# Output blocks and the next stage's first weights taken stream by stream; adaLN vectors summed on VectorE

## The chip, the cores and the metric

The kernel runs on one core of one Trainium2 chip. The metric is the device time of one execution in microseconds (us). Of the kernel before, three runs are shown: 2384.11, 2387.55 and 2390.22 us, median 2387.55 us.

## The reference, cut to what matters

The network has two layers over 512 tokens of width 1024: 256 latent tokens (called stream 0 here) and 256 context tokens (stream 1). A layer is a feed-forward block (FFN), a token mixer with three branches, and a second FFN; after each of them comes a LayerNorm of alpha * h + w * gate * f(u). Its input is modulated by adaLN vectors, nine per stream and layer, which are a matrix product of the conditioning vector with `ada_w`.

```python
u = modulate(h, mod[0], mod[1])                    # u * (1 + scale) + shift
a, b = split(u @ w_in); y = (silu(a) * b) @ w_out  # FFN, 2816 hidden columns
h = layer_norm(alpha * h + 0.5 * gate * y, g, b)   # mean and variance over the 1024 features of a token
```

In the last layer the context stream ends after the mixer's projections, so from there on only 256 tokens are computed.

## The kernel before, in words

Activations lie with features on the 128 partitions and tokens along the free axis: `u` is eight pairs of tiles (high part `uh`, low part `ul`, 128 x 512), one pair for each 128 features. Each product in float32 precision is three TensorE matmuls: weight high by `u` high, weight low by `u` high, weight high by `u` low (`mm3`, lines 139 to 143, and `projO`, lines 523 to 535). A weight of 128 x 1024 comes by one DMA into one of three `raw` buffers; `wload` (lines 120 to 133) splits it into a high part on ScalarE (line 130) and a low part on VectorE (line 132), into rings of three buffers each.

`ffn` (line 466) runs twice over 11 of the 22 blocks of hidden columns; for each block it multiplies two weights (line 530 and on), applies silu and product (lines 476 and 477), and after the 11 blocks it multiplies the eight output blocks `d` (line 516), 33 matmuls each over all 512 tokens. `residual` (line 361) adds each output block to `ah` and, in the second half, adds up the sum `s1` and the sum of squares `s2` over the features.

`norm` (line 391) then needs the sums over all eight blocks. Its TensorE work is written in a fixed order behind the last output matmul (`manual_schedule`, line 414): sums over the partitions by one-column matmuls (`token_mean`, line 388), the mean spread over all partitions (line 423), and 1/std spread by `bcast` (line 457). ScalarE, VectorE and GpSimd make the variance and the power (lines 424 to 426), VectorE subtracts the mean (line 411) and multiplies by 1/std (line 438), `mod` modulates (lines 348 to 352), `low` makes the low part (line 357), GpSimd makes the next `ah` (line 449). Only then can the next stage's first weights be multiplied. I call the stretch from the last output matmul to the first of those matmuls a hole; there are six norms: after FFN, mixer, FFN in layer 0 and the same in layer 1.

The adaLN vectors fill the holes. `ada_w` is cut into 18 groups of 512 columns per layer. `ada_group` (line 286) multiplies a group on TensorE, eight matmuls with the vector as the stationary operand, four transposes and a reduction (lines 293, 321, 322); `HOLES` says how many pieces go where in `norm`, and three groups stand in most holes. `ada_pairs` (line 250) does two groups in another way, in the background of an FFN: VectorE adds up weight times scalar (line 266, 28 instructions a pair), TensorE adds over the partitions (line 273) and transposes. `pull` (line 171) hands out the background's steps after blocks, `SKIP` leaves the first three out. The first three weights after a hole (the heads) share their steps over the eight `k`: each step has six matmuls by `uh` and then three by `ul`.

All loads go out on SyncE's queue (SP). The order of what is not fixed by hand is set by a scheduler at build time.

## Time and profile before

| | us |
|---|---|
| median of three runs | 2387.55 |
| the profiled execution, its own time | 2383.82 |
| its span, first to last instruction | 2382.0 |
| mean granted TensorE clock, share of full | 0.994 |

The profiled execution lies 3.7 us below the median, its span 1.8 us below its own time. A page counts the busy time of each engine, slices the span in 40, and lists groups of instructions; views of the trace give instructions in order of time. A matmul's row gives its time from start to end; successive matmuls overlap, so what one costs is read from the distance of two starts.

### The profile page before, as it was taken

The page shows a single profiled execution, that of the slowest core. Times are in us where ns is not written, and L with a number is a line of the kernel's source. Part 1 is how long each engine was busy: PE and PEld are TensorE (multiplying, and loading weights), DVE is VectorE, ACT ScalarE, POOL GpSimd, SP SyncE. Part 2 cuts the span into 40 slices and gives each one's busy share as a digit, 9 for nine tenths or more (in the row PEclk, how much of TensorE's full clock was granted, in tenths as well). Part 3 has the DMA queues.
Part 4 walks back from the last instruction along what each step waited for, and adds up shares of the span by engine and source line. Part 5 has one row for each costly group of instructions (what it writes and reads, how often), then busy time and mean ns, then how long its engine had stood idle before and what let it go on. Part 6 is the DMA issues. An engine that isn't in the chain of part 4 may idle for free.

```text
span 2382.0 us, 34116 instructions
## 1 busy us (share of the span) xinstructions
PE 2343.4 (98%) x13112; PEld 1971.4 (83%) x13112; DVE 1440.5 (60%) x2403; ACT 970.3 (41%) x1663; POOL 170.3 (7%) x158
## 2 busy tenths in 40 slices
PE   8999999999999999999999999999999999999998
PEld 4778778699888888867888877878887999998998
DVE  3647848656877665776433357363346687776555
ACT  3424324444654433343222234222225466645443
POOL 1003002210010000010000001000002111000000
PEclk9999999999999999999999999999999999999999
DMA  9435734723223445765332247243224344694564
GB/s 365 139 102 172 233 97 121 263 67 105 77 80 128 154 137 190 254 207 156 108 121 93 83 139 251 90 149 106 92 86 137 118 129 138 197 320 153 171 198 125
DMA packets 153314, 360.41 MB, mean 151 GB/s; under 512 B 16576, under 2 KB 38208, under 8 KB 153152
## 3 DMA queue, kind: packets, MB, share of 16 engines
q1 hardware_dynamic: 153152, 358.24, 46.2%
q8 instruction: 103, 1.69, 0.3%
q14 instruction: 59, 0.48, 0.1%
HBM read 331.96 MB, written 26.21 MB: 150 GB/s over the span
## 4 chain that ended last, share of the span: by engine, by line
PE 94%; DMA 2%; DVE 2%; ACT 1%; issue 1%; SPq 1%; POOL 0%; ACTq 0%; DVEq 0%
PE pj L530 18%; PE pj L531 18%; PE pj L533 18%; PE pj L141 7%; PE pj L143 7%; PE pj L142 7%; PE ph L632 2%; PE pj L551 1%; PE pj L552 1%; PE pj L553 1%; PE ph L293 1%; PE pa L1006 1%; PE pa L873 1%; PE ph L678 1%; PE pa L997 1%
## 5 line engine op out<-in xcount | busy, mean ns | idle before, releaser
L132 DVE TENSOR_TENSOR lo<-raw,hi 128x1024 fp32r<-128x1024 f32 (+1 forms) x455 | 524.6, 1154 | 451.1 <-ACT hi L130 450.2
L530 PE MATMUL pj<-uh,hi 128*128 128x512 f32 (+1 forms) x2096 | 752.5, 359 | 4.6 <-ACT uh L352 3.0
L533 PE MATMUL pj<-ul,hi 128*128 128x512 f32 (+1 forms) x2096 | 749.2, 358 | 1.1 <-DVE ul L357 1.1
L531 PE MATMUL pj<-uh,lo 128*128 128x512 f32 (+1 forms) x2096 | 749.5, 358 | 0.0
L130 ACT ACTIVATE hi<-raw 128x1024 fp32r<-128x1024 f32 (+1 forms) x455 | 446.4, 982 | 602.3 <-issue 251.2
L530 PEld LDWEIGHTS pj<-uh,hi 128*128 128x128 f32 x2096 | 396.6, 189 | 74.5 <-issue 8.6
L533 PEld LDWEIGHTS pj<-ul,hi 128*128 128x128 f32 x2096 | 396.1, 189 | 59.3 <-DVE ul L357 2.5
L531 PEld LDWEIGHTS pj<-uh,lo 128*128 128x128 f32 x2096 | 396.4, 189 | 56.8 <-issue 2.1
L142 PE MATMUL pj<-g,hi 128*128 128x512 f32 (+1 forms) x704 | 255.7, 363 | 0.0
L143 PE MATMUL pj<-g,lo 128*128 128x512 f32 (+1 forms) x704 | 255.5, 363 | 0.0
L141 PE MATMUL pj<-g,hi 128*128 128x512 f32 (+1 forms) x704 | 255.4, 364 | 0.0
L141 PEld LDWEIGHTS pj<-g,hi 128*128 128x128 f32 x704 | 132.8, 189 | 23.7 <-issue 1.7
L143 PEld LDWEIGHTS pj<-g,lo 128*128 128x128 f32 x704 | 132.9, 189 | 22.3 <-DVE ah L366 1.7
L142 PEld LDWEIGHTS pj<-g,hi 128*128 128x128 f32 x704 | 132.9, 189 | 21.3 <-issue 0.8
L476 ACT ACTIVATE silu<-pj 128x512 f32<-128x512 f32 (+1 forms) x87 | 47.3, 543 | 244.2 <-PE pj L533 244.2
L266 DVE SCALAR_TENSOR_TENSOR acc<-adaw,sc,acc 128x512 f32<-128x512 f32 x196 | 138.2, 747 | 3.9 <-DMA adaw<-ada_w 3.5
L477 DVE TENSOR_TENSOR silu<-silu,pj 128x512 f32<-128x512 f32 (+1 forms) x83 | 51.3, 619 | 147.0 <-PE pj L533 135.7
L366 DVE SCALAR_TENSOR_TENSOR ah<-pj,hg,ah 128x256 f32<-128x256 f32 x136 | 60.3, 478 | 90.0 <-PE pj L143 70.3
L426 POOL TENSOR_TENSOR rstd<-var,mhalf 128x4 f32<-128x4 f32 (+1 forms) x6 | 6.4, 1063 | 1111.9 <-DVE var L425 1111.9
L551 PE MATMUL pj<-hi,uh 128*128 128x256 f32 x288 | 82.2, 288 | 0.2
L552 PE MATMUL pj<-lo,uh 128*128 128x256 f32 x288 | 81.9, 286 | 0.0
L553 PE MATMUL pj<-hi,ul 128*128 128x256 f32 x288 | 81.6, 286 | 0.0
(293 smaller groups left out, 3110.3 us busy)
## 6 DMA issues: line engine op xcount, KB each, us to landing
raw<-ffn_in SPq DMA_DIRECT2D x176, 512.0 KB, 3.4
adaw<-ada_w SPq DMA_DIRECT2D x256, 256.0 KB, 4.8
raw<-mix_w SPq DMA_DIRECT2D x124, 512.0 KB, 3.5
raw<-ffn_out SPq DMA_DIRECT2D x64, 384.0 KB, 3.1
raw<-ffn_out SPq DMA_DIRECT2D x64, 320.0 KB, 2.9
raw<-branch_w SPq DMA_DIRECT2D x24, 512.0 KB, 5.3
adaw<-ada_f SPq DMA_DIRECT2D x32, 256.0 KB, 6.0
raw<-out_w SPq DMA_DIRECT2D x16, 512.0 KB, 4.6
```

The lines of the kernel that those rows point to most:

```text
L130: nc.scalar.activation(hi[:, :n], raw[:, :n], AF.Copy)
L132: nc.vector.tensor_tensor(lo[:, :n], raw[:, :n], hi[:, :n], ALU.subtract)
L141: nc.tensor.matmul(out, lhsT=wh, rhs=xh, start=start, stop=False)
L142: nc.tensor.matmul(out, lhsT=wh, rhs=xl, start=False, stop=False)
L143: self.last_mm = nc.tensor.matmul(out, lhsT=wl, rhs=xh, start=False, stop=stop)
L266: nc.vector.scalar_tensor_tensor(t, w, c, t, ALU.mult, ALU.add)
L530: self.nc.tensor.matmul(p, lhsT=hi, rhs=u[k][0][:, :n], start=(k == 0), stop=False)
L531: self.nc.tensor.matmul(p, lhsT=lo, rhs=u[k][0][:, :n], start=False, stop=False)
L533: self.last_mm = self.nc.tensor.matmul(p, lhsT=hi, rhs=u[k][1][:, :n], start=False, stop=(k == KD - 1))
L551: nc.tensor.matmul(o, lhsT=u[k][0][:, s], rhs=hi[:, c], start=(k == 0), stop=False)
L552: nc.tensor.matmul(o, lhsT=u[k][0][:, s], rhs=lo[:, c], start=False, stop=False)
L553: nc.tensor.matmul(o, lhsT=u[k][1][:, s], rhs=hi[:, c], start=False, stop=(k == KD - 1))
```

## The change

The five constants for the holes and the background are replaced. At four of the six norms (after layer 0's first FFN, its mixer, its second FFN, and layer 1's first FFN) a new function `seam` takes the place of the last output blocks, `norm`, and the matmuls of the next stage's first three weights. It multiplies the last two (FFN) or three (mixer) output blocks for stream 0, then for stream 1, and makes stream 0's sums, mean and 1/std between the matmuls of stream 1; then it multiplies the three weights for stream 0 and, between them, makes the sums of stream 1, and then for stream 1. The matmuls have 256 columns in place of 512. TensorE, VectorE and ScalarE follow the order written in `seam`. The weights of the last output blocks lie in the `U` buffers. The adaLN groups of these four holes, and group 15 of both layers, go to `ada_pairs`, which now takes five units in layer 0's first FFN and four in each of the next two; one unit sums four groups of the last layer for the latent stream alone. One `filters` call goes from the first to the second FFN. The two norms that stay get another order of their pieces.

```diff
-PAIR0 = ((6, 7), (8, 9), (13, 14))
-HOLES = (3, 0, 0, 2)
-BG = (2, 1)
 LAG = 4
-SKIP = (1, 2, 3)
+SKIP = 3
+PULL = (2.0, 1.5)
+STATS = 5
+SEAM = {mybir.EngineType.PE, mybir.EngineType.DVE, mybir.EngineType.Activation}
...
+    def wlast(self, src, n):
+
+        r = []
+        raw = self.raw()
+        self.nc.sync.dma_start(out=raw[:, :n * P], in_=src)
+        for c in range(0, n, 4):
+            m = min(4, n - c) * P
+            hi, lo = self.slab("U", F32R, "wh"), self.slab("U", F32R, "wl")
+            self.split(raw[:, c * P:c * P + m], hi[:, :m], lo[:, :m])
+            r += [(hi[:, k:k + P], lo[:, k:k + P]) for k in range(0, m, P)]
+        return r
...
+    def begin(self, bg, units):
+
+        self.bg, self.units, self.slot, self.due = bg, units * (8 + LAG + 1), 0, 0.0
+
...
         self.slot += 1
-        if self.slot not in self.bg_skip:
-            for _ in range(n):
-                next(self.bg, None)
+        if self.slot <= SKIP:
+            return
+        self.due += n
+        while self.due >= 1.0:
+            self.due -= 1.0
+            next(self.bg, None)
...
+        for part in gs:
+            ns = 4 // len(part)
...
+                acc += [self.slab("W", name="acc") for _ in range(ns)]
...
-                    for t, s in zip(acc[-2:], range(2)):
+                    for t, s in zip(acc[-ns:], range(ns)):
...
-                    if k % 2:
+                    if k % (4 // ns) == 4 // ns - 1:
                         yield
...
             p = self.pbank("ph")
-            for q, t in enumerate(acc):
-                nc.tensor.matmul(p[32 * q:32 * q + 32, :], lhsT=self.ones, rhs=t, start=True, stop=True,
-                                 tile_position=(0, 32 * q))
+            with self.tc.manual_schedule(engines={mybir.EngineType.PE}):
+                for q in (3, 2, 1, 0):
+                    nc.tensor.matmul(p[32 * q:32 * q + 32, :], lhsT=self.ones, rhs=acc[q], start=True, stop=True,
...
-            v = tr.rearrange("p (b g s x) -> p g b s x", b=4, g=2, s=2)
-            for i, g in enumerate(pair):
+            v = tr.rearrange("p (b g s x) -> p g b s x", b=4, g=len(part), s=ns)
+            for i, g in enumerate(part):
                 bias = self.par("ada_b", l * 72 + g * 4, 4)
-                nc.vector.tensor_tensor(mods[:, g * 4:g * 4 + 4, :], v[:, i, :, :, 0],
-                                        bias.unsqueeze(2).to_broadcast([P, 4, 2]), ALU.add)
+                x = v[:, i, :, :, 0] if ns == 2 else v[:, i, :, :, 0].to_broadcast([P, 4, 2])
+                nc.vector.tensor_tensor(mods[:, g * 4:g * 4 + 4, :], x, bias.unsqueeze(2).to_broadcast([P, 4, 2]), ALU.add)
...
-            more(HOLES[0])
-            for tb in range(nb):
-                self.token_mean(st["stat"][:, tb:tb + 1], st["s1"], tb, False, False)
-            more(HOLES[1])
-            for tb in range(nb):
-                self.token_mean(st["stat"][:, 4 + tb:5 + tb], st["sq"], tb, False, tb == nb - 1)
-            more(HOLES[2])
+            self.squares(st, TT)
+            for x, o, e in ((st["sq"], 4, True), (st["s1"], 0, False)):
+                for tb in range(nb):
+                    self.token_mean(st["stat"][:, o + tb:o + tb + 1], x, tb, False, not e and tb == nb - 1)
...
-            more(HOLES[3])
+            more(2)
             R = self.bcast(rstd, nb, "pa")
             more(100)
...
+        u += [self.low(x, TT) for x in pend]
+        self.ends = [x for x, _ in groups]
+        return u
+
+
+    def seam(self, l, prods, gate, ah, st, i, mods, ish, ws, ns):
+
+
+
+        nc = self.nc
+        G, B = self.affine(self.par("ln_g", l * 24 + i * 8, 8), self.par("ln_b", l * 24 + i * 8, 8), mods, ish, "n")
+        ws = [self.wlist(x) for x in ws]
+        rstd, mean, R, heads = [None] * 2, [None] * 2, [None] * 2, []
+        u = []
+        cols = lambda s: slice(s * L, (s + 1) * L)
+
+        def stats(s):
+            stat = self.pbank("pa")
+            x3 = (st["s2"], st["sq"][s], st["s1"])
+            for n, (x, o) in enumerate(zip(x3, (2, 2, 0))):
+                for tb in range(2):
+                    self.token_mean(stat[:, o + tb:o + tb + 1], x, (0 if n == 1 else 2 * s) + tb, n == 0 and tb == 0,
+                                    n == 2 and tb == 1)
+            mean[s] = self.pbank("pa")
+            nc.tensor.matmul(mean[s][:, :L], lhsT=self.onesD, rhs=st["s1"][:, cols(s)], start=True, stop=True)
+            msq, var, rstd[s] = (self.tiny(4, n, 2) for n in ("msq", "var", "rstd"))
+            nc.scalar.activation(msq[:, :2], stat[:, :2], AF.Square)
+            nc.vector.scalar_tensor_tensor(var[:, :2], stat[:, 2:4], LN_EPS, msq[:, :2], ALU.add, ALU.subtract)
+            nc.gpsimd.tensor_tensor(rstd[s][:, :2], var[:, :2], self.mhalf[:, :2], ALU.pow)
+
+        def center(d, s):
+            nc.vector.tensor_tensor(ah[d][:, cols(s)], ah[d][:, cols(s)], mean[s][:, :L], ALU.subtract)
+
+        def operand(d, s):
+
+            c, t = cols(s), ah[d][:, cols(s)]
+            if not s:
+                u.append((self.slab("U", F32R, "uh"), self.slab("U", F32R, "ul")))
+            uh, ul = u[d]
+            g, b = G[:, d, s:s + 1], B[:, d, s:s + 1]
+            x = self.slab("T", name="u")
+            nc.vector.tensor_tensor(t, t, R[s][:, :L], ALU.mult)
+            if d:
+                nc.scalar.activation(x[:, :L], t, AF.Identity, bias=b, scale=g)
+                h = nc.scalar.activation(uh[:, c], x[:, :L], AF.Copy)
+            else:
+                h = nc.scalar.activation(uh[:, c], t, AF.Identity, bias=b, scale=g)
+                nc.vector.tensor_scalar(x[:, :L], t, g, b, ALU.mult, ALU.add)
+            o = l * 24 + i * 8 + d
+            nc.gpsimd.tensor_scalar(t, t, self.alg[:, o:o + 1], self.alb[:, o:o + 1], ALU.mult, ALU.add)
+            yield
+            w = nc.vector.tensor_tensor(ul[:, c], x[:, :L], uh[:, c], ALU.subtract)
+            if s and d == 3:
+                self.marks = h, w
+            if s and d == KD - 1:
+                self.behind = h
+            yield
+
+        with self.tc.manual_schedule(engines=SEAM), self.tc.issue_after(self.last_mm.ins):
+            banks = []
+            for s in range(2):
+                n = 0
+                for d, ops in prods:
+                    p = self.pbank("pj")
+                    for k, (wh, wl, xh, xl) in enumerate(ops):
+                        self.mm3(p[:, :L], wh, wl, xh[:, cols(s)], xl[:, cols(s)], k == 0, k == len(ops) - 1)
+                        n += s
+                        if n == STATS:
+                            stats(0)
+                        elif STATS < n <= STATS + KD:
+                            center(n - STATS - 1, 0)
+                        elif n == STATS + KD + 1:
+                            R[0] = self.bcast(rstd[0], 2, "pa")
+                    if not s or d < KD - 1:
+                        self.residual_of(d, p, gate, ah, st, s)
+                last = p
+            for s in range(2):
+                w = ws[:ns[s]]
+                banks = [self.pbank(t) for t in (("pj", "pj", "ph"), ("pj", "ph", "pa"))[s][:ns[s]]]
+                x = [operand(k, s) for k in range(KD)]
+                next(x[0])
+                for k in range(KD):
+                    if k < KD - 1:
+                        next(x[k + 1])
+                    next(x[k])
+                    xh, xl = u[k][0][:, cols(s)], u[k][1][:, cols(s)]
+                    for y, p in zip(w, banks):
+                        nc.tensor.matmul(p[:, :L], lhsT=y[k][0], rhs=xh, start=(k == 0), stop=False)
+                        nc.tensor.matmul(p[:, :L], lhsT=y[k][1], rhs=xh, start=False, stop=False)
+                    for y, p in zip(w, banks):
+                        self.last_mm = nc.tensor.matmul(p[:, :L], lhsT=y[k][0], rhs=xl, start=False, stop=(k == KD - 1))
+                        self.tick(L)
+                    if not s:
+                        if k == 0:
+                            self.residual_of(KD - 1, last, gate, ah, st, 1)
+                        elif k == 2:
+                            stats(1)
+                        elif 2 < k < KD - 1:
+                            center(2 * k - 6, 1)
+                            center(2 * k - 5, 1)
+                        if k == 5:
+                            R[1] = self.bcast(rstd[1], 2, "pa")
+                heads.append(banks)
+        return u, heads
+
+    def residual_of(self, d, y, gate, ah, st, s):
+
+        nc = self.nc
+        c = slice(s * L, (s + 1) * L)
+        nc.vector.scalar_tensor_tensor(ah[d][:, c], y[:, :L], gate[:, d, s:s + 1], ah[d][:, c], ALU.mult, ALU.add)
+        sq = self.slab("T", name="sq")
+        a = nc.scalar.activation(sq[:, :L], ah[d][:, c], AF.Square)
+        self.marks = a, nc.vector.tensor_tensor(st["s1"][:, c], st["s1"][:, c], ah[d][:, c], ALU.add)
+        if d < KD - 1:
+            nc.vector.tensor_tensor(st["s2"][:, c], st["s2"][:, c], sq[:, :L], ALU.add)
+        else:
+            st.setdefault("sq", {})[s] = sq
+
+    def end_groups(self):
+        for x in self.ends:
+            next(x, None)
+        self.ends = []
...
+        hidden = 2 * HALF - (2 if pre else 1) - SKIP
+        rate = self.units / (PULL[0] * hidden + PULL[1] * (KD + 5))
...
+                elif n == 2 and heads:
+                    banks = [list(x) for x in zip(*heads)]
+                    w3 = self.wload(a["ffn_in"][l, i, jj + 1, 1], tags="FF", marks=self.marks)
+                    with self.tc.issue_after(self.behind.ins):
+                        finish(*banks[:2])
+                    banks = banks[2:] + self.projO([w3], u, [TT], "pa")
                 elif n == 2:
                     banks = self.projO([w(q) for q in range(3)], u, [TT] * 3)
                     finish(*banks[:2])
+                    self.end_groups()
                     banks = banks[2:] + self.projO([w(3)], u, [TT], "ph")
...
-                self.pull(BG[0])
+                self.pull(rate * PULL[0])
...
-                if half and d == KD - 1:
-                    self.squares(st, TT)
+                if half and seam and d == KD - 2:
+                    prods = []
+                    for dd in (d, d + 1):
+                        w = []
+                        for k0, k1 in ((0, 6), (6, HALF)):
+                            w += self.wlast(a["ffn_out"][l, i, half, dd][:, k0 * P:k1 * P], k1 - k0)
+                        prods.append((dd, [(*w[k], *g[k]) for k in range(HALF)]))
+                    return self.seam(l, prods, hg, ah, st, **seam)
...
-                self.pull(BG[1])
+                if d == 5 and half:
+                    for _ in self.bg:
+                        pass
+                elif d < 5 or not half:
+                    self.pull(rate * PULL[1])
...
+        if heads:
+            w3 = self.wload(self.a["mix_w"][l, i + 3], tags="FF", marks=self.marks)
+            pz = [[(x, slice(q * L, (q + 1) * L), slice(0, L)) for q, x in enumerate(b)] for b in zip(*(h[:2] for h in heads))]
+            pq = [(h[2], slice(q * L, (q + 1) * L), slice(0, L)) for q, h in enumerate(heads) if len(h) > 2]
...
+            with self.tc.issue_after(self.behind.ins) if heads else ExitStack():
+                for b, o, e in pz[r]:
+                    nc.scalar.activation(f[:, c][:, o], b[:, e], AF.Sigmoid)
+                    nc.scalar.activation(k[:, c][:, o], b[:, e], AF.Sigmoid, scale=-1.0)
...
+        if heads:
+            pg = self.projO([w3], u, [NQ], "pa")[0]
...
-                self.squares(st, TT)
+            if seam and d == KD - 3:
+                prods = []
+                for dd in range(d, KD):
+                    w = self.wlast(self.a["out_w"][l, dd], KD)
+                    prods.append((dd, [(*w[k], *mm[k]) for k in range(KD)]))
+                return self.seam(l, prods, hg, ah, st, **seam)
...
         fill = {
             (0, 0): [lz(ada, 0, 4), lz(ada, 0, 5), None, self.tables_a] + [None] * F0 + [lz(self.filters, 0)] + [None] * F1 +
-                    [self.tables_b, lz(ada, 0, 15), lz(self.filters, 1)],
-            (1, 0): [None] + [lz(ada, 1, 15)],
+                    [self.tables_b],
+            (0, 1): [None] * 6 + [lz(self.filters, 1)],
         }
-        bg = {(0, 0): self.ada_pairs(0, PAIR0, mods[0]),
-              (0, 1): self.ada_pairs(1, [(1, 2), (3, 7)], mods[1]),
-              (1, 0): self.ada_pairs(1, [(8, 9), (13, 14)], mods[1])}
+        bg = {(0, 0): (0, [(6, 7), (8, 9), (12, 13), (14, 15), (10, 11)], 5),
+              (0, 1): (1, [(0, 1), (2, 3), (4, 5)], 4),
+              (1, 0): (1, [(6, 7), (8, 9), (10, 11, 12, 13), (14, 15)], 4)}
+
+        def background(l, i):
+            if (l, i) not in bg:
+                return self.begin(iter(()), 0)
+            k, gs, n = bg[l, i]
+            first = self.ada_pairs(0, [(16, 17)], mods[0]) if (l, i) == (0, 1) else ()
+            self.begin(itertools.chain(first, self.ada_pairs(k, gs, mods[k])), n)
+
+        def ffn_head(l, i):
+            return dict(ws=[a["ffn_in"][l, i, q // 2, q % 2] for q in range(3)], ns=(3, 3))
...
+            last = l == DEPTH - 1
+            background(l, 0)
+            u, heads = self.ffn(l, 0, u, ah, T, lambda: self.mod_cols(mods[l], 2), fill.get((l, 0)), None if l else pre, heads,
+                                dict(i=0, mods=mods[l], ish=3, ws=[a["mix_w"][l, 4 + q] for q in range(3)],
+                                     ns=(3, 2 if last else 3)))
+            r = self.mixer(l, u, heads, ah, TT, self.mod_cols(mods[l], 5),
+                           None if last else dict(i=1, mods=mods[l], ish=6, **ffn_head(l, 1)))
+            u, heads = r if not last else (self.norm(l, 1, ah, TT, r, mods[l], 6, fill=[(l, g, mods[l]) for g in (16, 17)]),
+                                           None)
+            background(l, 1)
+            r = self.ffn(l, 1, u, ah, TT, lambda: self.mod_cols(mods[l], 8), fill.get((l, 1)), None, heads,
+                         None if last else dict(i=2, mods=mods[l + 1], ish=0, **ffn_head(l + 1, 0)))
+            if last:
+                self.norm(l, 2, ah, TT, r, None, 0, out=self.out)
             else:
-                self.norm(l, 2, ah, TT, st, None, 0, out=self.out)
+                u, heads = r
```

## Rows read from the trace of the kernel before

**Rows 1.** The page: busy time by engine; granted clock in 40 slices, tenths.

```profile
PE 2343.4 (98%) x13112; PEld 1971.4 (83%) x13112; DVE 1440.5 (60%) x2403; ACT 970.3 (41%) x1663; POOL 170.3 (7%) x158
...
PEclk9999999999999999999999999999999999999999
```

**Rows 2.** Timeline of TensorE, second FFN, 512 columns: start, length, what; 19 matmuls apart.

```profile
1099.68 0.39 PE L530 MATMUL pj<-uh,hi 128*128 128x512 f32 x1
...
1103.99 0.39 PE L531 MATMUL pj<-uh,lo 128*128 128x512 f32 x1
```

**Rows 3.** Timeline of TensorE, last FFN, 256 columns; 24 matmuls apart.

```profile
2229.81 0.28 PE L531 MATMUL pj<-uh,lo 128*128 128x256 f32 x1
...
2232.69 0.28 PE L531 MATMUL pj<-uh,lo 128*128 128x256 f32 x1
```

**Rows 4.** Timeline of TensorE: last output matmul and first head matmul, four holes.

```profile
441.31 0.39 PE L143 MATMUL pj<-g,lo 128*128 128x512 f32 x1
...
462.06 0.50 PE L530 MATMUL pj<-uh,hi 128*128 128x512 f32 x1
...
1034.20 0.39 PE L533 MATMUL pj<-m,hi 128*128 128x512 f32 x1
...
1051.22 0.50 PE L530 MATMUL pj<-uh,hi 128*128 128x512 f32 x1
...
1419.60 0.39 PE L143 MATMUL pj<-g,lo 128*128 128x512 f32 x1
...
1434.87 0.51 PE L530 MATMUL pj<-uh,hi 128*128 128x512 f32 x1
...
1802.80 0.39 PE L143 MATMUL pj<-g,lo 128*128 128x512 f32 x1
...
1818.07 0.51 PE L530 MATMUL pj<-uh,hi 128*128 128x512 f32 x1
```

**Rows 5.** Stretches: busy us of PE, PEld, DVE, ACT, POOL; clock, DMA share, GB/s.

```profile
440.00:462.00 22.00, 18.00 (x98) 8.41 (x96) 12.94 (x23) 7.92 (x13) 4.99 (x5) 0.84 0.83 297
1051.00:1078.00 27.00, 24.56 (x108) 19.39 (x107) 27.00 (x45) 13.37 (x23) 8.27 (x5) 1.00 0.65 216
```

**Rows 6.** The chain that ended last: start, us, what, in two FFN stretches.

```profile
1423.78 1.88 PE pa L389 x16
1425.66 0.97 PE pa L423 x2
...
1428.99 0.89 PE pa L461 x8
1429.88 1.93 PE ph L293 x16
...
1557.98 1.00 PE ph L273 x8
```

**Rows 7.** Timeline of TensorE, third hole: the transposes of one adaLN group.

```profile
1432.45 0.66 PE L321 MATMUL ph<-prm,ada 128*128 128x128 f32 x4 [0.71 <-ACT ada L318]
```

**Rows 8.** VectorE by line and form: count, busy us, mean ns, idle before.

```profile
L132 DVE TENSOR_TENSOR lo<-raw,hi 128x1024 fp32r<-128x1024 f32 x327 | 406.5, 1244 | 345.5 <-ACT hi L130 344.9
L266 DVE SCALAR_TENSOR_TENSOR acc<-adaw,sc,acc 128x512 f32<-128x512 f32 x196 | 138.2, 747 | 3.9 <-DMA adaw<-ada_w 3.5 <-ACT acc L264 0.4
...
L366 DVE SCALAR_TENSOR_TENSOR ah<-pj,hg,ah 128x256 f32<-128x256 f32 x136 | 60.3, 478 | 90.0 <-PE pj L143 70.3 <-PE pj L533 19.4
...
L357 DVE TENSOR_TENSOR ul<-u,uh 128x256 fp32r<-128x256 f32 x8 | 3.3, 424 | 1.1 <-ACT uh L352 1.1
...
L438 DVE TENSOR_TENSOR t<-t,pa 128x256 f32<-128x256 f32 x8 | 3.1, 414 | 1.3 <-PE pa L461 1.3
```

**Rows 9.** ScalarE by line and form, same columns.

```profile
L130 ACT ACTIVATE hi<-raw 128x1024 fp32r<-128x1024 f32 x327 | 345.2, 1057 | 348.8 <-issue 192.5 <-PE pj L142 53.3 <-PE pj L533 43.4
...
L350 ACT ACTIVATE u<-t,B,G 128x256 f32<-128x256 f32 x64 | 35.3, 591 | 23.2 <-DVE t L438 21.9 <-DVE ul L357 1.1
...
L352 ACT ACTIVATE uh<-u 128x256 fp32r<-128x256 f32 x8 | 3.1, 410 | 0.1
```

77 lines of the change are left out of this document (35 added, 42 removed).

## The prediction

> **What bounds it now.** I read the page first. TensorE is busy for 98% of the span and VectorE for 60% [rows 1], so only what shortens TensorE's own list, or its few idle stretches, can show; and a busy TensorE may be doing work that need not be there. The clock slices [rows 1] are full, though a short stretch can hide in one. Next the timeline, for what a matmul costs by the distance of starts: 4.31 us over 19 matmuls of 512 columns, 0.227 us each [rows 2]; 2.88 us over 24 matmuls of 256 columns, 0.120 us each [rows 3]. So two halves cost 0.240 and a whole 0.227: 0.0132 us for each matmul cut in two.
>
> Then the four holes that the change closes [rows 4]. From the start of the last output matmul to that of the first head matmul, less the 0.23 us of the former, they last 20.5, 16.8, 15.0 and 15.0 us, together 67.4. In the first TensorE is busy for 18.0 of 22 us at a mean granted clock of 0.84 [rows 5], so part of it runs at 1.2 and not 2.4 GHz. What fills a hole is mostly adaLN work: a group costs 1.93 us for its matmuls and about 0.5 for its transposes [rows 6, 7]. After the second hole comes a stretch of 27 us with TensorE busy 24.56 and VectorE busy throughout [rows 5]: VectorE's queue, not only the hole, is late there.
>
> **What the change takes away.**
> - The four holes: 67.4 us.
> - The transposes of the third group, which stand behind the hole: four times about 0.4 = 1.6 [rows 7], whose 0.66 includes the tail of the last one.
> - Group 15 of both layers, until now TensorE work within an FFN: 2 x 2.45 = 4.9 [rows 6, 7].
> - The waits behind the second hole: 27 - 24.56 = 2.4 [rows 5]. One is for a silu that frees a bank; the heads are now followed by the fourth weight in another bank, 24 x 0.227 = 5.4 us of cover [rows 2], where the whole wait behind the hole was 2.4.
>
> Sum 76.3.
>
> **What it adds to TensorE.**
> - Sums, mean and spreading are still needed: per seam 12 one-column matmuls at 1.88 / 16 = 0.12 [rows 6], 1.4; two means of 256 columns, together between 0.97 and 1.2, I take 1.1; spreading 0.89 [rows 6]. That is 3.4, less the four of 0.12 that stood outside the hole: 2.9, four times 11.6.
> - Cuts: two FFN output blocks have 66 matmuls, three mixer blocks 72, three weights 72 (the last seam 48, as its third weight has one stream before and after). 138 + 138 + 114 + 144 = 534, by 0.0132 = 7.1 us.
> - adaLN: 14 groups leave TensorE and six more units come to `ada_pairs`; each is 1.00 for its eight records and 0.5 for transposes [rows 6, 7]: 9.0.
>
> Sum 27.7, so 48.6 us are won if TensorE never waits in a seam.
>
> **What it will wait.** The seam's order is fixed on three engines, so each is a queue in which one late instruction holds up all behind it. I lay its instructions beside TensorE's 72 x 0.120 = 8.6 us of heads.
> - Stream 0's sums come after five products of stream 1's first block, 15 x 0.12 = 1.8 us after stream 0's last matmul; the residual, 0.48, and a sum of 0.42 come before them [rows 8]. That fits. So does the chain of variance and power behind nine more products, 3.2 us.
> - Heads of stream 0: VectorE has 24 instructions of about 0.42 (multiplication, low part, stream 1's centring) [rows 8], the residual and its sum 0.9, one modulation 0.6, together 11.5 us. TensorE has 8.6 + 1.7 of stream 1's sums = 10.3. VectorE is 1.2 over. And the variance waits for ScalarE's square of the mean while two instructions for the next operands stand behind it: about 1.8 more. 3.0.
> - Heads of stream 1: ScalarE has 8 x (0.59 + 0.41) [rows 9] and the next weight's high part, 1.06: 9.1 against 8.6. The first operand's chain, 0.41 + 0.59 + 0.42 = 1.4 [rows 8, 9], is half covered. 1.5.
>
> So 4.5 a seam and 18.0 for four. Below, the cost is nothing; above, a chain of 1.84 us a step (0.41, 0.59, 0.41, 0.42) with three hand-overs, 2.0 us, against 9 x 0.12 = 1.08: 16 x 0.92 = 14.7 a seam. I stay near the lower end, since the code starts operand k + 1 before it ends k.
>
> The background brings VectorE six units of 28 x 0.747 = 21 us [rows 8], 126 in all: 1440 becomes 1566 of 2382, 66%. It is spread over three FFNs in which the page shows TensorE full, and is covered by the weights' splits running up to three buffers ahead; without that cover a lost low part costs up to 1.24 us [rows 8] per weight. Two seams are followed by a background; an instruction of it that slips into the seam costs up to 0.75. I take 2.2 for both, like the waits found there [rows 5], with 0 below and 24 above (one a step, 32 steps).
>
> For nothing I take these. The 112 `ada_w` loads of the 14 groups keep their size and go out on SP between weight loads, no longer in a burst at a hole; DMA was at 0.83 there [rows 5]. `filters` moves from an FFN to another, under its matmuls. The splits for `wlast` come in smaller pieces, under the blocks before. GpSimd makes the next `ah` in 16 pieces a seam and not 8, while it is busy for 7% of the span [rows 1]. The `hd` copies wait for GpSimd as before. The two norms that stay move three pieces of 0.48 us (a quarter of a group [rows 6]) behind the spreading: 1.4 us either way.
>
> **Sum.** 48.6 - 18.0 - 2.2 = 28.4. The profiled execution of 2383.8 becomes 2355.4; on the median, which is 3.7 higher, 2359.
>
> **A rule against it.** TensorE starts a matmul every 0.120 us although a weight load's row is 0.19 us long in this trace, and PEld is busy for 83% of the span [rows 1, 3]: loads run beside matmuls. The Trainium skill, TensorE: Matmul & The Clock Gate, Part 3 (the mechanism), says that a weight load overlaps matmuls in flight only if it goes to another group of rows; here every load uses all 128 rows, so by it each cut would cost a load. By that page's figure, 128 / 1.2 = 107 ns, I estimate 534 x 0.107 = 57 us, more than all that is won. The trace does not agree: 0.120 us for 256 columns leaves no room for it [rows 3].
>
> **The rivals.**
> - *The seam runs serially (slower).* If the operands' steps do not overlap, because a `T` buffer is not free (six; two hold sums, one or two squares), each seam loses 14.7: 48.6 - 58.8 - 2.2 = -12, 2400 us. It decides from (48.6 - 2.2) / 4 = 11.6 us a seam. Against it: two operands in flight need two buffers, and at least two are left. 0.05.
> - *Weight loads show (slower).* By the rule above, worked from the rows: 534 cuts, each with a further load of 0.19, 101 us; 2460. The distance of starts speaks against it. 0.01.
> - *The background takes the seam (no change).* VectorE is full behind the second hole [rows 5]. One background step in each step of two seams costs 24 in place of 2.2, net 6.6: 2381. For it: the scheduler fills idle moments of VectorE, and only the seam's own instructions are tied to one another. 0.08.
> - *The seams lose 7 to 10 us each* by GpSimd and VectorE disturbing each other or by banks held: net 7 to 18, 2375. 0.11.
> - *Hardly a wait.* Under 1 us a seam, net 45: 2343. 0.12.
>
> **How the numbers follow.** My forecast, 2 to 7 us a seam, has 0.63. About 0.3%, 7 us, is what a measurement of this kernel can tell from no change. Faster by more: 0.63 + 0.11 + 0.12 = 0.86. Within: 0.08. Slower: 0.06. The range goes from 2339 (48.6 won in full) to 2381, which leaves out the slower cases and part of the rest.
>
> **What would show it.** `ada_group` matmuls (line 293 now) fall from 288 records to 64. TensorE goes without a break of over 1 us from the last output blocks into the heads, at the full clock, matmuls of 256 columns 0.12 us apart; its waits in a seam add up to some 4 us, mostly for `ul` (VectorE) in stream 0 and for `uh` (ScalarE) in stream 1. VectorE's busy time rises by about 130 us. I am wrong if waits in a seam pass 10 us, if TensorE begins to wait for low parts of weights inside the FFNs, or if starts of 256 columns stand further apart than 0.12.

## The result, and the profile after

The changed kernel takes 2404.05 us (median of 7 runs, 2396.51 to 2408.66). The kernel before, beside it on the same chip, takes 2385.95 (7 runs, 2380.66 to 2390.22). The ratio is 1.0073, 95% interval 1.0053 to 1.0093: the change loses some 18 us where I forecast 28 won. The profiled execution spans 2406.3 us.

The page of the changed kernel: busy time, and the granted clock in 40 slices.

```profile
PE 2326.2 (97%) x13446; PEld 2002.3 (83%) x13446; DVE 1555.0 (65%) x2688; ACT 996.2 (41%) x1752; POOL 180.4 (7%) x194
...
PEclk9999899999999999999979999999999999999999
```

Against [rows 1], TensorE is busy for 17 us less, yet the span is 24 us longer: what came in is idle TensorE. VectorE rose by 114.5 us. Two slices of the clock are no longer full. Where TensorE waited (line, who released it; us in all, times, longest):

```profile
PE ph L302 <- DVE acc L294: 28.1, 2, 14.5
PE pj L160 <- DVE ah L395: 8.9, 1, 8.9
...
PE pj L160 <- DVE gate L1233: 5.6, 4, 2.8
PE ph L308 <- ACT ada L305: 5.0, 2, 2.5
PE pa L418 <- DVE sq L592: 4.2, 1, 4.2
```

Line 302 is the sum over the partitions of one background unit (line 273 before), line 294 VectorE's running sum for it (266 before). The row left out is a wait of 5.8 at the start, which the kernel before has too. Of the rows shown only the last, for the squares, stands in a seam, the third. By stretches (columns as in [rows 5]), first the two that hold the waits, then seams 1 to 4:

```profile
225.00:275.00 50.00, 32.96 (x147) 25.52 (x146) 35.34 (x48) 14.77 (x20) 5.08 (x4) 0.84 0.90 309
1185.00:1215.00 30.00, 13.23 (x65) 9.25 (x63) 12.78 (x21) 7.14 (x12) 5.57 (x4) 0.70 0.92 319
```

```profile
430.00:475.00 45.00, 44.59 (x336) 42.08 (x335) 28.06 (x69) 24.25 (x52) 13.19 (x20) 1.00 0.28 93
1015.00:1060.00 45.00, 44.57 (x336) 42.00 (x334) 29.78 (x75) 22.75 (x46) 13.02 (x20) 1.00 0.08 24
1408.00:1475.00 67.00, 62.45 (x389) 55.68 (x388) 57.12 (x119) 29.35 (x54) 8.57 (x14) 0.95 0.45 142
1815.00:1850.00 35.00, 33.22 (x261) 31.56 (x260) 24.67 (x63) 16.68 (x33) 9.56 (x14) 1.00 0.26 82
```

The seams do what the change says. TensorE is idle for 0.41, 0.43, 4.55 and 1.78 us in them, where holes of 20.5, 16.8, 15.0 and 15.0 us stood [rows 4]; the 4.55 are mostly the wait of 4.2 for the squares. The loss is inside two FFNs. TensorE's timeline there, the last matmul before the sum and what followed it:

```profile
253.68 0.39 PE L704 MATMUL pj<-ul,hi 128*128 128x512 f32 x1
268.60 1.94 PE L302 MATMUL ph<-acc,ones 128*32 128x512 f32 x8 [14.54 <-DVE acc L294]
273.04 1.12 PE L308 MATMUL ph<-prm,ada 128*128 128x128 f32 x4 [2.50 <-ACT ada L305]
...
1208.74 1.94 PE L302 MATMUL ph<-acc,ones 128*32 128x512 f32 x8 [13.57 <-DVE acc L294]
1213.17 1.12 PE L308 MATMUL ph<-prm,ada 128*128 128x128 f32 x4 [2.50 <-ACT ada L305]
1223.21 0.80 PE L160 MATMUL pj<-g,hi 128*128 128x512 f32 x1 [8.92 <-DVE ah L395]
```

A sum of a microsecond of work holds up every FFN matmul behind it for 14.5 and 13.6 us. (The Trainium skill, TensorE: Matmul & The Clock Gate, Part 3, the mechanism, says that matmuls are strict first in, first out; by that rule a late matmul stops those behind it. The trace agrees.) In the second place the gate's groups 16 and 17, which before were summed in the hole ahead of this FFN, are this very unit. So the gate, the residuals and with them a bank are late too, 8.9 us more. After each wait some eleven matmuls start 0.43 us apart, the lower of the two clocks, before 0.23 returns.

The sum waits because its loads came late. SP's queue, the background's `ada_w` loads around that time, in the changed kernel:

```profile
221.57 3.11 SPq L288 DMA_DIRECT2D adaw<-ada_w  x6
...
226.74 0.33 SPq L288 DMA_DIRECT2D adaw<-ada_w  x1
...
229.87 2.22 SPq L288 DMA_DIRECT2D adaw<-ada_w  x5
...
240.83 0.99 SPq L288 DMA_DIRECT2D adaw<-ada_w  x1
```

The loads of an even `k` lie in ring E, those of an odd `k` in ring H. VectorE's first running sum needs an odd `k`, and its wait ends as the load of 240.83 lands, 6.8 us after that went out; DMA is at 0.90 in this stretch, and how much that adds was not tried apart. From there VectorE needs 20.9 us for the unit's 28 sums and two low parts of weights:

```profile
247.63 4.73 DVE L294 SCALAR_TENSOR_TENSOR acc<-adaw,sc,acc 128x512 f32<-128x512 f32 x7 [2.09 <-DMA adaw<-ada_w]
...
253.42 5.38 DVE L294 SCALAR_TENSOR_TENSOR acc<-adaw,sc,acc 128x512 f32<-128x512 f32 x8
...
259.85 8.70 DVE L294 SCALAR_TENSOR_TENSOR acc<-adaw,sc,acc 128x512 f32<-128x512 f32 x13
```

In the second FFN it is a single late load, behind the last stores of `filters`, for which VectorE's last two sums of the unit wait:

```profile
1201.86 0.76 SPq L288 DMA_DIRECT2D adaw<-ada_w  x1
```

```profile
1207.28 1.41 DVE L294 SCALAR_TENSOR_TENSOR acc<-adaw,sc,acc 128x512 f32<-128x512 f32 x2 [10.83 <-DMA adaw<-ada_w]
```

The loads of the first FFN's unit in the kernel before, and its sums on TensorE:

```profile
223.25 2.70 SPq L260 DMA_DIRECT2D adaw<-ada_w  x6
...
243.38 2.24 SPq L260 DMA_DIRECT2D adaw<-ada_w  x4
```

```profile
270.78 1.04 PE L273 MATMUL ph<-acc,ones 128*32 128x512 f32 x2
...
272.65 1.04 PE L273 MATMUL ph<-acc,ones 128*32 128x512 f32 x2
...
279.29 1.04 PE L273 MATMUL ph<-acc,ones 128*32 128x512 f32 x2
...
282.09 1.05 PE L273 MATMUL ph<-acc,ones 128*32 128x512 f32 x2
```

So the loads were as late before: the unit's buffers come from the rings that `filters` uses (E, H), and the loads stand behind those of `filters`, which is called first. No wait told of it, since with three units in this FFN the sum stood at 270 to 282. With five units it stands at 254. That is the theory which the runs below had to try.

### The profile page after: what moved, and what is told of

It reads as the page before. It is cut to its first block, busy times and chain, and to the rows that moved or that the text cites. A ratio compares the mean times of both kernels' runs of the same rounds, so it can differ in the third digit from the quotient of the medians.

```text
span 2406.3 us, 35191 instructions
## 1 busy us (share of the span) xinstructions
PE 2326.2 (97%) x13446; PEld 2002.3 (83%) x13446; DVE 1555.0 (65%) x2688; ACT 996.2 (41%) x1752; POOL 180.4 (7%) x194
## 4 chain that ended last, share of the span: by engine, by line
PE 88%; DVE 5%; DMA 3%; ACT 2%; issue 1%; SPq 0%; POOL 0%; ACTq 0%; DVEq 0%; POOLq 0%
PE pj L701 17%; PE pj L702 17%; PE pj L704 17%; PE pj L160 7%; PE pj L161 7%; PE pj L162 7%; DVE acc L294 2%; PE ph L810 2%; PE pj L723 1%; PE pj L724 1%; PE pj L722 1%; PE pa L1184 1%; PE pa L1051 1%; PE ph L856 1%; PE pa L1175 1%
## 5 line engine op out<-in xcount | busy, mean ns | idle before, releaser
L134 DVE TENSOR_TENSOR lo<-raw,hi 128x1024 fp32r<-128x1024 f32 (+2 forms) x444 | 515.7, 1163 | 380.3 <-ACT hi L132 379.5
L701 PE MATMUL pj<-uh,hi 128*128 128x512 f32 (+1 forms) x2064 | 740.8, 359 | 2.8 <-ACT uh L381 2.8
L702 PE MATMUL pj<-uh,lo 128*128 128x512 f32 (+1 forms) x2064 | 737.7, 357 | 0.0
L704 PE MATMUL pj<-ul,hi 128*128 128x512 f32 (+1 forms) x2064 | 737.1, 358 | 0.0
L132 ACT ACTIVATE hi<-raw 128x1024 fp32r<-128x1024 f32 (+2 forms) x444 | 437.4, 987 | 591.3 <-issue 237.8
L294 DVE SCALAR_TENSOR_TENSOR acc<-adaw,sc,acc 128x512 f32<-128x512 f32 x364 | 252.6, 746 | 22.2 <-DMA adaw<-ada_w 14.3
L160 PE MATMUL pj<-g,hi 128*128 128x512 f32 (+1 forms) x638 | 231.3, 363 | 8.9 <-DVE ah L395 8.9
L161 PE MATMUL pj<-g,hi 128*128 128x512 f32 (+1 forms) x638 | 230.6, 362 | 0.0
L162 PE MATMUL pj<-g,lo 128*128 128x512 f32 (+1 forms) x638 | 230.4, 362 | 0.0
L160 PEld LDWEIGHTS pj<-g,hi 128*128 128x128 f32 x638 | 120.9, 190 | 30.6 <-DVE ah L395 9.3
L162 PEld LDWEIGHTS pj<-g,lo 128*128 128x128 f32 x638 | 121.1, 190 | 18.2
L161 PEld LDWEIGHTS pj<-g,hi 128*128 128x128 f32 x638 | 121.1, 190 | 18.0
L631 ACT ACTIVATE silu<-pj 128x512 f32<-128x512 f32 (+1 forms) x87 | 46.3, 533 | 209.5 <-PE pj L704 202.9
```

Of the source, the lines that this page charges most:

```text
L132: nc.scalar.activation(hi[:, :n], raw[:, :n], AF.Copy)
L134: nc.vector.tensor_tensor(lo[:, :n], raw[:, :n], hi[:, :n], ALU.subtract)
L160: nc.tensor.matmul(out, lhsT=wh, rhs=xh, start=start, stop=False)
L161: nc.tensor.matmul(out, lhsT=wh, rhs=xl, start=False, stop=False)
L162: self.last_mm = nc.tensor.matmul(out, lhsT=wl, rhs=xh, start=False, stop=stop)
L294: nc.vector.scalar_tensor_tensor(t, w, c, t, ALU.mult, ALU.add)
```

## The experiments

All ratios are to the kernel before, timed beside each on the same chip (its medians: 2384.91, 2385.18, 2386.51 and 2384.74 us in the four groups below).

**First group: is it the buffers, the number of units, or the seams?**

*Separate buffers.* The background loads into ring p, and `filters` uses E wherever it used p.

```diff
-                    w = self.slab("EH"[k % 2], name="adaw")
+                    w = self.slab("p", name="adaw")
-        mlp = self.slab("p", name="mlp")
+        mlp = self.slab("E", name="mlp")
...
```

> Only the buffers differ: the background's ada_w blocks go into the ring p alone, and filters, which used p, E and H, now uses E and H alone, so neither waits for the other's buffers. Theory A (the changed kernel loses by the late start of a background unit while filters holds the buffers, and TensorE then stands before that unit's sum over partitions): the two waits of line 302 for VectorE's sums (14.5 and 13.6 us) and what hangs on them (2.5, 2.5 and 8.9 us) are gone, with the stretches at the lower clock behind them: 2360 us (2350 to 2375). Theory B (VectorE has too many sums to make, wherever the blocks lie): waits of that size stay, 2404 us (2395 to 2412). Theory C (the seams lose): no change, 2404 us.

2353.9 us (2351.53 to 2355.68), ratio 0.988 (0.9865 to 0.9896): the loss of 18 becomes 31 won. Of the 16 loads of the first FFN's second unit, six now go out by 107 us and the others from 163.45 on, where the first of them stood at 221.57:

```profile
163.45 3.82 SPq L288 DMA_DIRECT2D adaw<-ada_w  x3
...
169.51 1.71 SPq L288 DMA_DIRECT2D adaw<-ada_w  x2
```

and no sum waits any more. The largest waits left of this kernel, besides one of 5.7 at the start:

```profile
PE pj L701 <- ACT uh L381: 2.8, 1, 2.8
PE pa L943 <- POOL ab L939: 2.6, 1, 2.6
PE pa L418 <- DVE sq L592: 2.2, 1, 2.2
```

*Few units.* Seams as in the change; the background has the seven units of before again, and the other groups run on TensorE within the FFNs. Buffers stay shared.

```diff
-        bg = {(0, 0): (0, [(6, 7), (8, 9), (12, 13), (14, 15), (10, 11)], 5),
+        bg = {(0, 0): (0, [(6, 7), (8, 9), (13, 14)], 3),
...
```

> The seams stay; the adaLN groups that the change took to VectorE are done on TensorE, one after a block of an FFN, and the seven pairs of the kernel before are the background. Theory A: the seams hardly wait, so without the background's waits (some 50 us in the changed kernel) about 2350, and 14 groups on TensorE at 2.45 us less six units at 1.5 us bring 25: 2375 us (2363 to 2383), faster than before. Theory C (the seams lose): 2400 us or more. Theory B: as A.

2368.74 (2366.73 to 2371.36), ratio 0.9944 (0.9928 to 0.9959), and no wait of a sum: shared buffers alone do no such harm.

*No seams.* All the sums on VectorE as in the change, norms with (now empty) holes.

> The other half alone: the adaLN groups go to VectorE as in the changed kernel, the four seams are replaced by the norms of the kernel before with nothing in their holes. Theory A: the same waits of line 302 and of the residual behind it, 40 to 50 us, in the first two FFNs; the holes shrink from 67 us to some 44, and 5.5 us less work elsewhere is offset by 9 more: about 2365 without waits, 2410 us with them (2398 to 2420). Theory C (the seams lose, the background does not): 2365 us (2358 to 2375).

2398.92 (2396.49 to 2401.61), ratio 1.007 (1.0054 to 1.0086). The sums wait for 17.3 us here too, and 8.9 for the residual. So the loss comes with the units, not with the seams.

*A longer distance* between a unit's last products and its sum, buffers shared.

```diff
-LAG = 4
+LAG = 8
```

> LAG 8 in place of 4: each unit's sum over partitions stands four background steps (about 23 us) further back in the program, while sums and buffers are as they were. Theory A: the wait of 14.5 us in the first FFN, where nothing hangs on the unit, goes away, that of the second FFN stays in some form since the gate of that FFN needs its first unit: 2385 us (2375 to 2398). Theory B: the waits move but stay, 2404 us (2397 to 2412).

2379.91 (2376.78 to 2384.47), ratio 0.9983 (0.9972 to 0.9995). One wait of 15.2 is left, in the first FFN; the one in the second is gone. Theory A had it the other way round, the first to go and the second to stay, so that its time (2375 to 2398) is met by luck.

**Second group: place in the queue, undoing one part, and a control.**

*Distance 16.*

```diff
-LAG = 4
+LAG = 16
```

> The changed kernel with 16 instead of 4 steps between a unit's last products and its sum over the partitions; buffers are shared as in the change. Theory A (the loss is the sum standing at a fixed place in TensorE's queue, while the unit's loads wait for buffers that the filter generation holds; nothing else is lost in the FFNs): the sum over partitions nowhere waits for VectorE, 0 to 3 us in place of 28.1, and the time is 2354 to 2366, I take 2360. Theory B (the late loads make VectorE's burst itself the loss: low parts of the weights come late behind it, whatever stands in TensorE's queue): the wait moves to low parts or residuals, and the time stays at 2375 to 2395. Theory C (with 16 steps the units no longer fit and the rest is drained at the end of the FFN, into the seam): the time is 2380 or more, with waits in the seams.

2380.27 (2378.36 to 2383.22), ratio 0.9981 (0.997 to 0.9993), a wait of 13.7 in the first FFN. None of my three theories said this, and the program explains it: steps are paced by the units' whole length, 8 + LAG + 1. The second unit's sum stands at step 25 of 65 with LAG 4, at 33 of 85 with 8 and at 49 of 125 with 16: always 0.38 to 0.39 of the way. LAG brings loads forward, it does not move the sum back. In the second FFN it was the first unit's loads that mattered, and they moved from step 8 of 52 to 8 of 68, ahead of `filters`.

*`filters` of layer 1 back at the end of the first FFN.*

```diff
-                    [self.tables_b],
-            (0, 1): [None] * 6 + [lz(self.filters, 1)],
+                    [self.tables_b, None, lz(self.filters, 1)],
```

> The changed kernel with the filter generation of layer 1 back at the end of layer 0's first FFN, where it was; buffers are shared as in the change. Theory A (the loss in the second FFN, 13.6 and 2.5 and 8.9 us and what the low clock behind it adds, comes from filters moved there): that loss goes, the one in the first FFN stays, and the time is 2372 to 2384, I take 2378; the second filter generation meets another unit at the end of the first FFN at a cost of at most 5. Theory B (the units there are the loss, filters or not): 2400 or more. Theory C (at its old place it stops one more unit in the first FFN, for another 13 us or more): 2388 to 2400.

2403.59 (2400.51 to 2404.54), ratio 1.0065 (1.005 to 1.008). Its waits (same columns as above):

```profile
PE ph L302 <- DVE acc L294: 29.5, 2, 15.8
```

Theory C names the place, though the time lies above its range (2388 to 2400), and theory B has the time without the place: no sum waits in the second FFN, but both waits are now in the first. This stretch (columns of [rows 5]) had no such wait in the changed kernel:

```profile
450.00:480.00 30.00, 11.19 (x53) 8.80 (x53) 17.18 (x34) 3.77 (x9) 0.73 (x1) 0.60 0.32 103
```

With the background at work throughout, `filters` met a unit at either place.

*Separate buffers, no seams,* and *the kernel before with separate buffers,* its edit that of the first experiment on either.

> The adaLN sums on VectorE as in the change, the norms with empty holes in place of the seams, and separate buffers for the background's loads and the filter generation. With the runs before it this makes a square: without both 2384.9, seams alone 2368.7, both 2353.9. Theory A (the two halves of the change add up once the buffers are apart: the seams are worth 16.2, the move of the sums 14.8): 2370, 2364 to 2376. Theory B (the move empties the holes, so that there is little left for a seam to win; the seam's two streams are worth under 5 us): 2354 to 2360. Theory C (an empty hole costs as much as one filled with groups, since nothing but the norm's chain decides its length): 2378 to 2386.

> The kernel before with separate buffers for the background's loads and the filter generation, and nothing else of the change. Theory A (before, the units were few and early enough not to meet the filter generation): 2385, within 3 us of the kernel before. Theory B (the buffers cost the kernel before something too, which the page did not show as a wait): 2365 to 2379; then part of what the separated version wins is not the change's.

Without seams 2365.08 (2364.59 to 2367.85), ratio 0.9906 (0.9889 to 0.9922), at the lower end of theory A's range (2364 to 2376). The kernel before with separate buffers takes 2374.65 (2374.04 to 2379.24), ratio 0.9951 (0.9935 to 0.9966): theory A fell. The sharing cost the kernel before 10 us, which its list of waits did not show. At equal numbers of projection columns (as in the table below) they come in three places: some 4 where the second unit's sums stand, 4 at the first hole and 3 behind the second; some are lost again later, and what became shorter there I did not follow. So of the 31 us that the separated version wins, 10 are not the change's. With buffers apart, moving the sums wins 2374.7 - 2365.1 = 9.6, and the seams on top of it 2365.1 - 2353.9 = 11.2. The first of these steps also brings the tie of the next group, so it is not shown for the move alone.

**Third group: the tie.** The change also put the four matmuls of a sum under a fixed order on TensorE; before, they were left to the scheduler. I took this for the cause, since a freed sum might wait without stopping others.

```diff
-            with self.tc.manual_schedule(engines={mybir.EngineType.PE}):
-                for q in (3, 2, 1, 0):
+            for q, t in enumerate(acc):
...
```

> The changed kernel with the four sums over the partitions of a unit placed freely among TensorE's matmuls, as the kernel before had them, and no longer tied together at a fixed place; buffers are shared as in the change. Theory A (the tie is what turns late loads into idle TensorE: what waits for VectorE must not stand in front of matmuls that are ready): no wait of these sums for VectorE over 2 us, in place of 28.1, and the time falls to 2362 to 2382, I take 2372; against the version with separate buffers some 10 us are still lost, since the scattered sums take about 2 us a unit and not 1, and since the gate still comes late in the second FFN. Theory B (the late loads themselves are the loss, because the weights' low parts queue behind the burst on VectorE): the waits move to low parts, 2390 or more.

> The kernel before with the sums over the partitions tied together at a fixed place as in the change, and nothing else. Theory A (the tie makes idle time wherever a unit's loads come late, and in the kernel before the second unit's products ran in a burst from 255 to 298 us too): TensorE waits there for VectorE for 5 to 15 us, less 1 us saved a unit on seven units: 2378 to 2395, I take 2388. Theory B (the tie only saves the scattering, since the few units of the kernel before are in time): 2376 to 2380, without a wait.

> The changed kernel with separate buffers and, besides, the sums over the partitions placed freely. With loads in time there is nothing to wait for, so the tie can only save. Theory A (scattered sums cost about 1 us more a unit, thirteen units): 2361 to 2369, I take 2365, against 2353.9 with the tie. Theory B (the tie saves nothing where the loads are in time): 2352 to 2358.

The changed kernel without the tie: 2401.61 (2399.79 to 2403.1), ratio 1.007 (1.0055 to 1.0085). Its sums (one line further up) wait as before:

```profile
PE ph L301 <- DVE acc L294: 24.8, 3, 12.5
PE pj L160 <- DVE ah L394: 5.8, 1, 5.8
```

Theory A fell, and theory B has the time (2390 or more) but not the waits, which did not move to low parts. A freed sum too has one place in TensorE's list, and waits there. The kernel before with the tie: 2377.5 (2375.5 to 2380.52), ratio 0.9969 (0.9956 to 0.9982), so there the tie gains 9 us; counted from start to start, the sums of its seven units take 7.9 us in place of 14.7, which makes 6.8 of the 9. With separate buffers and no tie: 2353.39 (2351.27 to 2354.52), ratio 0.9867 (0.985 to 0.9883), no different from 2353.9 with it: the sums take 17.8 and not 13.9 us, but that comes back elsewhere. Theory B held for both.

*The background held out of the seam,* on the version with separate buffers: the first pass of the next FFN's units on ScalarE waits for the seam's last operand.

```diff
                         if k == 0:
-                            nc.scalar.activation(t, w, AF.Copy, scale=c)
+                            with self.tc.issue_after(tie.ins) if tie else ExitStack():
+                                nc.scalar.activation(t, w, AF.Copy, scale=c)
...
+            tie = self.behind if (l, i) != (0, 0) else None
```

> The version with separate buffers (2353.9) in which the first pass of the next FFN's background on ScalarE also waits for the seam's last operand, so that its sums on VectorE cannot run in the seam. Theory A (sums in the third seam make the residual and the squares late): the wait of the token sums for the squares, 2.2 us, goes, the window of the third seam has 1 to 2 us without a matmul in place of 3.5, and the time is 2349 to 2353, I take 2351. Theory B (the sums are then late in the next FFN, whose gate and norm need them): 2355 or more. Within 0.1% the times cannot tell these apart; the windows and waits have to.

2345.12 (2343.46 to 2350.03), ratio 0.9837 (0.9821 to 0.9853), the best version of all. The third seam's window without the hold and with it:

```profile
1375.00:1445.00 70.00, 66.51 (x427) 59.23 (x426) 57.35 (x117) 32.77 (x62) 11.66 (x18) 0.98 0.40 132
```

```profile
1375.00:1445.00 70.00, 69.54 (x445) 62.41 (x444) 55.51 (x111) 34.71 (x63) 11.66 (x18) 1.00 0.42 131
```

3.5 us without a matmul become 0.5, and the wait for the squares is gone. Theory A held on the place and expected too little (2349 to 2353): at equal numbers of projection columns the two kernels are 4.5 us apart already in the first FFN, which the hold does not touch, 5 come at this seam and 2.5 near the end (1.6 are lost in between). The first 4.5 arise between 202 and 210 us: there the version without the hold waits 2.6 us for `ab` (its list above) and then starts seven matmuls some 0.43 us apart; with the hold this wait is absent. Why, the runs do not show, so about half of the 8.8 us that this version wins over the one without the hold is not shown to be the hold's.

**Fourth group: only the order of the program.** Buffers shared and sums tied as in the change. A pause of one unit's length stands behind the first unit of the first FFN, and `filters` comes five blocks later in the second.

```diff
-            (0, 1): [None] * 6 + [lz(self.filters, 1)],
+            (0, 1): [None] * 11 + [lz(self.filters, 1)],
...
+                rest = itertools.chain(self.ada_pairs(0, gs[:1], mods[0]), itertools.repeat(None, 8 + LAG + 1),
+                                       self.ada_pairs(0, gs[1:], mods[0]))
```

> The changed kernel with nothing altered but the order of the program: in the first FFN of layer 0 a pause of one unit's length (13 steps) stands between the first and the second unit, and in its second FFN the filter generation comes five blocks later, so that the first unit's loads stand ahead of it. Buffers stay shared and the sums stay tied. Theory A (the loss is a collision in the program's order: more units bring a unit's sum nearer, while its loads still wait for the filter generation's buffers; in the kernel before they went out as late, from 223 us, and the sum stood further back): the sums wait for VectorE 0 to 4 us in place of 28.1, some 15 us come back in the first FFN and some 30 in the second, and the time is 2354 to 2372, I take 2362. Theory B (buffers shared by the filter generation and the background cost TensorE wherever both stand in one FFN): another unit's sum waits instead, 2385 or more.

2383.61 (2379.16 to 2387.39), ratio 0.9994 (0.9984 to 1.0004): 20 us better than the change. The second unit's loads still go out as late, and its sum, now further back, waits for nothing:

```profile
217.89 5.65 SPq L288 DMA_DIRECT2D adaw<-ada_w  x6
```

```profile
275.76 1.06 PE L302 MATMUL ph<-acc,ones 128*32 128x512 f32 x8
```

In the second FFN the first unit is free, and the third one has taken its place:

```profile
1293.87 5.44 SPq L288 DMA_DIRECT2D adaw<-ada_w  x6
```

```profile
1329.88 1.94 PE L302 MATMUL ph<-acc,ones 128*32 128x512 f32 x8 [14.01 <-DVE acc L294]
```

Neither range is met: theory A said 2354 to 2372 with 0 to 4 us of waits, theory B 2385 or more. In the first FFN theory A holds, a collision in the program's order that the order removes; in the second I only moved it, and another unit's sum waits, as theory B said. To follow this I noted when each kernel has started the same number of projection columns (all have 4.5 million). Against the version with separate buffers, the lag in us is:

| after | changed kernel | spaced |
|---|---|---|
| 0.37 million columns (217 us) | -0.4 | -0.4 |
| 0.47 million (268 us) | 14.8 | -7.9 |
| 0.84 million (448 us, seam 1) | 13.5 | -4.9 |
| 2.16 million (1162 us) | 15.8 | -1.3 |
| 2.25 million (1206 us) | 46.3 | -3.7 |
| 2.53 million (1333 us) | 46.3 | 24.8 |
| 2.72 million (1432 us, seam 3) | 48.6 | 27.3 |
| all | 52.4 | 31.4 |

Two places make nearly all of the 52 us: some 15 in the first FFN and 30.5 in the second. (Just ahead of the first stop, at 0.45 million, the changed kernel was 6 us in front, so the stop itself costs some 21.) In the first, 14.5 and 2.5 are listed waits; in the second 13.6, 2.5 and 8.9 make 25.0. The matmuls at 0.43 us stand behind them. (The other entries move a little as small pieces of work change places.)

*The missing corner of the square:* seams, few units, separate buffers (the edits of the first two experiments together).

> The seams with the adaLN work as TensorE had it (within the FFNs), and with separate buffers: the last corner of the square with separate buffers, of which neither is 2374.7, the move alone 2365.1, both 2353.9. Theory A (the two halves add up): 2374.7 - 11.2 = 2363.5, 2360 to 2367. Theory B (seams and moved sums each win the same time, the groups' work in the holes; the seams alone then win most of it): 2354 to 2359. Theory C (separate buffers bring this version nothing, since its units are few): 2367 to 2371, as with shared buffers.

The median is 2375.92, ratio 0.9966 (0.9952 to 0.9979), but the runs go from 2365.4 to 2378.49, a spread of 13 us at nearly the same clock (0.997 and 0.995 in the first two), and the profile is of the fastest. That is inconclusive: the profiled execution fits theory A, the median none. How the win splits between seams and moved sums is thus known along one path only.

## Why the prediction was wrong

- **The failed step** is a sentence of the waits and one of the list of things "for nothing". I had the background "covered" by the weights' splits running ahead, and let `filters` move "under its matmuls". I priced VectorE's 126 us as work, and the units' sums as TensorE time (1.00 each), but never asked from which ring the loads come, who holds it, and what stands behind the sum in TensorE's queue. That wait costs 28.1 us directly, and with what hangs on it 45 of the 52 us between the changed kernel and the one with separate buffers, net.
- **The gate.** Groups 16 and 17 moved out of a hole to a unit at the head of the very FFN whose gate needs them. I counted that as one of six units. It added 8.9 us.
- **The cover I named was the wrong one.** I looked for late low parts of weights; their waits are 0.7 and 0.3 us here. VectorE at 65% was no bound over the whole, though the stopped unit's 28 sums took it 20.9 us.
- **The seams were right, and better than priced.** I took 4.5 us of waits each; it was 0.41, 0.43, 4.55 and 1.78, together 7.2 and not 18.0. Two were "hardly a wait". The third is mostly the next FFN's sums slipping in, the mechanism that I priced at 2.2; holding them out gave 3.0 us in its window.
- **TensorE's own sum held roughly.** With separate buffers the kernel comes to 2353.9 where I said 2359, but by errors that cancel: 10 us of that are what separate buffers give any version, so the change itself is worth 2374.7 - 2353.9 = 20.8 and not 28.4. By distances of starts, the projections took 26.9 us more in this version than in the kernel before (2060.1 to 2087.0), where cuts were priced at 7.1; what the cuts cost by themselves no run shows. The rest holds the seams' waits, 5.6 us of pauses over 0.5 us near 202 and 238 us beside `filters`, and many small delays of under 0.5 us, which I had no term for. The tie, which I did not price, saved 1 us a unit in the kernel before.
- **The rivals.** "Seam runs serially" gave 2400, near the result, for a reason that is not there. "The background takes the seam" had the right culprit in the wrong place: it took the FFNs. Full overlap of weight loads was right: matmuls of 256 columns in the seams stand 0.12 us apart.
- **The signs.** VectorE rose by 114.5 us (I said 130) as [rows 8] grew from 196 to 364 sums, and `ada_group` matmuls fell to 64 records as forecast; I had the sign that TensorE begins to wait inside the FFNs, but for low parts, not for the sums.

## What to carry to other kernels

A step that moves to an idle engine still has an end on the busy one: find the instruction with which it comes back, its place in that queue, and everything that must be done by then, down to the buffers of its loads. More steps in the same stretch bring that place nearer even if nothing else changes, so slack that was ample for three units can be negative for five. Where independent work shares a ring of buffers, the part that comes first in the program holds the other's loads; separating the rings was worth more here than any timing knob.

## What the runs showed that I had not expected

- Lateness can be there and cost nothing visible: loads at 223 us before, at 221 after, and the difference is 14.5 us of idle TensorE.
- The kernel before lost 10 us to shared buffers, though its largest wait by line, besides one at the start, is 9.7 us for the transposes of adaLN groups, and that one stays with separate buffers (10.1). The list of waits is no list of what can be won.
- Leaving the order of the sums free did not help: 24.8 us of waits against 28.1 with the tie.
- An idle stretch of TensorE costs more than its length: eleven matmuls or so at 0.43 and not 0.23 us, about 2 us, followed each of the two stops.
